# Two FFN stages of a diffusion layer: four raw weight buffers, later stores, resident output weights, and sums spread over the next product

## The chip, the cores and the metric

The kernel runs on one core of one Trainium2 chip. The core has TensorE (PE, with its weight loads shown apart as PEld), VectorE (DVE), ScalarE (ACT), GpSimd (POOL) and SyncE (SP), which here issues the DMA transfers. The time is device microseconds of one execution; a kernel's time is the median of several runs. Each kernel also has one execution with the hardware profiler on, and all rows of a profile belong to that execution.

## The reference

One layer for 1,024 latent tokens (x_sample) and 256 context tokens (x_prompt), model width 1,024, in float32. Two gated FFNs of inner width 2,816 stand around a token-mixing step; the change touches the FFNs only.

```python
def swiglu(h, w_in, w_out):
    gate, up = jnp.split(h @ w_in, 2, axis=-1)
    return (jax.nn.silu(gate) * up) @ w_out

def layer(x, cond, p, ...):
    ...
    h = rms_norm(x, p['norm_ffn1']) * (1.0 + sc1) + sh1
    x = x + 0.5 * g1 * swiglu(h, p['w_ffn1_in'], p['w_ffn1_out'])
    h = rms_norm(x, p['norm_mix']) * (1.0 + sc2) + sh2
    mix, k_ctx, v_ctx, s_ctx = token_mix(h, p, ...)
    x = x + g2 * mix
    h = rms_norm(x, p['norm_ffn2']) * (1.0 + sc3) + sh3
    x = x + 0.5 * g3 * swiglu(h, p['w_ffn2_in'], p['w_ffn2_out'])
```

w_in is 1,024 x 5,632, w_out 2,816 x 1,024. The vectors sh, sc and g come from the conditioning.

## The kernel before

Activations lie with the model dimension on the 128 partitions, eight tiles of 128 rows (`x[c][d]`); the tokens are three chunks: c = 0 and 1 are the latents (512 each), c = 2 is the prompt (256). Each float32 operand is split into a high part (`copy` to fp32r on ScalarE) and a low part (`subtract` on VectorE or GpSimd), and each product is three matmuls: high by high, high by low, low by high (`mm3`, line 129). So every weight tile is loaded, cast, subtracted, and only then used.

The program is written with a tile framework that finds the dependencies, allocates buffers by tag and puts each engine's instructions into an order of its own: by the order of the program among what is ready. It can issue a transfer long before the place where it is written, but each engine's queue, SP's too, is then run in that fixed order. A pool opened in the place of a closed one takes over its memory. Only the attention part is pinned to program order. `K.side` holds generators of side work (norms, operand splits, outputs); `tick` (line 114) advances each by one step between pieces of the main work.

One FFN (`ffn`, line 1392) has four stages.

1. *Prompt in* (`prompt_in`, line 468). For each of the NF = 22 tiles of inner width it takes a gate weight tile (g, 1,024 x 128, 512 KB) and an up tile (u), makes 24 matmuls of 256 columns with each, applies Silu on ScalarE, multiplies on VectorE, and stores the result s to DRAM (`gp_d`) for the fourth stage. Weights come by `wload` (line 88): raw tile (tag wr, two buffers), cast by ScalarE to wh, low part wl by VectorE (g) or GpSimd (u), four buffers each. `ahead(2)` keeps two converted tiles ready. Side work meanwhile makes the operands of the latents.
2. *Latents in* (`in_blocks` line 514, `latents_in` line 555). The latents' product is a 2 x 2 block scheme with seven products in place of eight (`prod`). For p = 0 to 10 (NPR = 11 pairs of inner tiles) and gate and up (u = 0, 1), it makes the seven products on operand tiles that stay on chip in pool `hp` (tags hh0, hl0, hh1, hl1, hh2, hl2) and in the x buffers, then seven combinations per pair are stored to DRAM (`g_d`). The weight blocks of this stage lie in pool `fp`.
3. *Latents out* (`out_blocks` line 623, `latents_out` line 656). Seven products again, in the order i = 1, 2, 5, 6, 7, 4, 3. Each runs over the 11 pairs p; a pair is 12 matmuls of 512 columns into four PSUM banks. For each pair a raw tile of two halves is loaded: g (256 KB of `g_d`) and a (256 KB of w_out), with a second piece of w_out for i = 5 and 7 (tag wr2). Products 5, 6, 7 and 3 use sums or differences of weight quarters. The raw tile is in tag wr (two buffers, kept through the kernel) or, for every third, wr3 in this stage's own pool `op`. `block` (line 488) casts and splits each half: a on GpSimd, g on VectorE. After a product, all its sums into x (`scalar_tensor_tensor`, one of 512 columns per bank and quarter of x, 4 to 16 per product) are written one behind the other; where a quarter of x is final, `done` starts its sum of squares (FFN1) or its output (FFN2). x itself was stored to DRAM while its memory held operands, and is loaded again before this stage: 4 MB of the latents, and 1 MB of the prompt's (`x_move`, tile xr).
4. *Prompt out* (`prompt_out_blocks` line 679, `prompt_out` line 692). For each of 22 tiles: w_out rows (512 KB), v (the stored s), split both, 24 matmuls of 256 columns.

After FFN1 comes the mixing step with its own projections, which also take their weights by `wload`.

## Time and profile before

| what | us |
|---|---|
| median of 3 runs | 2931.68 (2926.15 to 2934.43) |
| the profiled execution | 2935.67, span 2933.8 |
| FFN1: prompt in, latents in, latents out, prompt out start at | 41.6, 229.9, 705.7, 964.6 |
| FFN2: the same | 2022.8, 2187.4, 2615.4, 2862.4 |
| last matmul of FFN2's prompt out | 2927.7 |

Starts are those of the stage's first matmul, from the span's start. VectorE is busy for 1628.4 us of the span, GpSimd for 1265.5, ScalarE for 1122.1. A row of the timeline gives start, duration, engine, operation, the tiles written and read, and in brackets how long the engine had stood before it and what ended that. In names, numbers of buffers are left out: ffn2w_3g is the g block of pair 3 in any of the seven products, ffn2w_3b its weight block, ffn2w_3r the raw tile, ffn2u12r, h and l are raw, high and low part of up tile 12.

### The profile page before, as it was taken

The numbers are of one execution on the slowest core, as the hardware profiler recorded it, in microseconds if no ns is written. First come the engines' busy times: TensorE is split into PE (matmuls) and PEld (weight loads), VectorE is DVE, ScalarE is ACT, GpSimd is POOL, SyncE is SP. The second block draws the span as 40 slices with busy tenths as digits, with TensorE's granted clock in tenths as the row PEclk, the third lists the DMA queues.
The fourth block names the chain that finished last, engine by engine and source line by source line (L and its number), as shares of the span: only waits on it lengthen the run. The fifth ranks groups of instructions, "written<-read, shape, count | busy, mean of one in ns | idle before, by whom it ended". The sixth has DMA issues, their size and how long they took to land.

```text
span 2933.8 us, 44077 instructions
## 1 busy us (share of the span) xinstructions
PE 2732.8 (93%) x17070; PEld 2359.7 (80%) x17070; DVE 1628.4 (56%) x2162; ACT 1122.1 (38%) x1892; POOL 1265.5 (43%) x902
## 2 busy tenths in 40 slices
PE   6889999998989899999998999999889999989899
PEld 5776667886767798999988888888777888867789
DVE  4824344554676735464646388737525555546654
ACT  5532223332434533232323477735332333323344
POOL 2334334443445646455655112165335444434443
PEclk8999999999999899999999999999999999999999
DMA  8556664335665541313132954375553333256665
GB/s 300 164 156 193 208 205 140 108 101 191 220 196 197 184 156 48 110 58 107 54 98 84 222 116 110 129 248 158 151 147 93 108 108 108 90 195 217 202 215 194
DMA packets 420600, 446.62 MB, mean 152 GB/s; under 512 B 21549, under 2 KB 315685, under 8 KB 417317
## 3 DMA queue, kind: packets, MB, share of 16 engines
q1 hardware_dynamic: 420208, 443.73, 48.5%
q8 instruction: 134, 2.20, 0.3%
q14 instruction: 78, 0.63, 0.1%
q10 hardware_dynamic: 180, 0.06, 0.0%
HBM read 344.09 MB, written 99.61 MB: 151 GB/s over the span
## 4 chain that ended last, share of the span: by engine, by line
PE 63%; DVE 9%; DMA 8%; POOL 5%; issue 4%; ACT 2%; SPq 1%; DVEq 0%; ACTq 0%; POOLq 0%
PE mob L49 3%; PE ffn2po L49 3%; PE ffn2pp L49 2%; PE ffn1po L49 2%; PE ffn1pp L49 2%; PE hi0b L49 1%; PE ak1b L49 1%; PE ak0b L49 1%; PE aq0b L49 1%; PE ada L49 1%; PE av1b L49 1%; PE hi1b L49 1%; PE hg1b L49 1%; PE hg0b L49 1%; SPq L49 1%
## 5 line engine op out<-in xcount | busy, mean ns | idle before, releaser
L49 PE MATMUL ffn1pp<-ffn1pvv,ffn1pw 128*128 128x256 f32 x528 | 69.2, 295 | 4.6 <-ACT ffn1pvv L49 4.6
L49 PEld LDWEIGHTS ffn1pp<-ffn1pvv,ffn1pw 128*128 128x128 f32 x528 | 68.0, 203 | 5.8 <-ACT ffn1pvv L49 4.9
L49 PE MATMUL ffn2pp<-ffn2pvv,ffn2pw 128*128 128x256 f32 x528 | 64.0, 283 | 0.0
L49 PEld LDWEIGHTS ffn2pp<-ffn2pvv,ffn2pw 128*128 128x128 f32 x528 | 63.6, 192 | 0.1
L49 PE MATMUL ada<-wada,cst 128*32 128x256 f32 x448 | 39.8, 395 | 4.0 <-DMA wada<-w_ada 3.9
L49 POOL TENSOR_TENSOR ffn2pw<-ffn2pw,ffn2pw 128x512 fp32r<-128x512 f32 x22 | 28.9, 1316 | 33.6 <-ACT ffn2pw L49 29.7
L49 POOL TENSOR_TENSOR ffn1pw<-ffn1pw,ffn1pw 128x512 fp32r<-128x512 f32 x22 | 31.2, 1424 | 21.0 <-ACT ffn1pw L49 20.9
L49 PE MATMUL ffn1po<-ffn1w_3g,ffn1w_3b 128*128 128x512 f32 x84 | 25.7, 453 | 11.9 <-DVE ffn1w_3g L49 11.9
L49 DVE TENSOR_TENSOR sacc<-sacc,sq 128x512 f32<-128x512 f32 (+1 forms) x18 | 27.0, 1500 | 15.7 <-ACT sq L49 15.5
L49 ACT CAST ffn1pw<-ffn1pw 128x512 fp32r<-128x512 f32 x44 | 25.8, 616 | 23.2 <-DMA ffn1pw<-w_ffn_out 21.4
L49 PE MATMUL ffn1po<-ffn1w_2g,ffn1w_2b 128*128 128x512 f32 x84 | 23.5, 430 | 11.9 <-ACT ffn1w_2b L49 11.6
L49 ACT CAST ffn2pw<-ffn2pw 128x512 fp32r<-128x512 f32 x44 | 26.8, 620 | 18.1 <-DMA ffn2pw<-w_ffn_out 12.0
L49 PE MATMUL ffn2po<-ffn2w_2g,ffn2w_2b 128*128 128x512 f32 x84 | 23.4, 427 | 11.0 <-ACT ffn2w_2b L49 10.7
L49 PE MATMUL ffn2po<-ffn2w_3g,ffn2w_3b 128*128 128x512 f32 x84 | 24.3, 439 | 9.2 <-DVE ffn2w_3g L49 9.2
L49 POOL TENSOR_TENSOR hl<-nt,hh 128x256 fp32r<-128x256 f32 (+1 forms) x20 | 22.5, 1127 | 24.0 <-ACT hh L49 24.0
L49 ACT ACTIVATE nt<-nt,mt,sv 128x256 f32<-128x256 f32 (+1 forms) x40 | 25.5, 681 | 18.8 <-DVE nt L49 11.5
L49 PEld LDWEIGHTS ffn1po<-ffn1w_3g,ffn1w_3b 128*128 128x128 f32 x84 | 18.2, 223 | 18.0 <-DVE ffn1w_3g L49 14.0
L49 DVE TENSOR_TENSOR ffn2pw<-ffn2pw,ffn2pw 128x512 fp32r<-128x512 f32 x22 | 18.0, 817 | 25.9 <-ACT ffn2pw L49 25.9
L49 PEld LDWEIGHTS ffn1po<-ffn1w_2g,ffn1w_2b 128*128 128x128 f32 x84 | 17.0, 207 | 17.2 <-ACT ffn1w_2b L49 12.0
L49 PEld LDWEIGHTS ada<-wada,cst 128*32 128x32 f32 x448 | 9.8, 108 | 25.7 <-issue 19.3
L49 PEld LDWEIGHTS ffn2po<-ffn2w_2g,ffn2w_2b 128*128 128x128 f32 x84 | 16.7, 206 | 16.0 <-ACT ffn2w_2b L49 11.1
L49 DVE TENSOR_TENSOR ffn1pw<-ffn1pw,ffn1pw 128x512 fp32r<-128x512 f32 x22 | 20.6, 936 | 16.1 <-ACT ffn1pw L49 13.6
(4022 smaller groups left out, 10296.8 us busy)
## 6 DMA issues: line engine op xcount, KB each, us to landing
wada<-w_ada SPq DMA_DIRECT2D x112, 256.0 KB, 3.0
ffn1r<-w_ffn_in SPq DMA_DIRECT2D x44, 512.0 KB, 4.3
ffn2r<-w_ffn_in SPq DMA_DIRECT2D x44, 512.0 KB, 3.8
ffn1pw<-w_ffn_out SPq DMA_DIRECT2D x22, 512.0 KB, 4.5
ffn2pw<-w_ffn_out SPq DMA_DIRECT2D x22, 512.0 KB, 3.3
g_d<-ffn1t SPq DMA_DIRECT2D x33, 256.0 KB, 2.8
g_d<-ffn2t SPq DMA_DIRECT2D x33, 256.0 KB, 2.9
wadb<-w_ada SPq DMA_DIRECT2D x12, 512.0 KB, 8.8
```

What stands on the lines that cost most here:

```text
L49: r = f(*a, **k)
```

## The change

In the prompt stage, raw weight tiles come from four buffers, two of wr and two of a new tag wrx in another pool, with up to three loads issued ahead of their cast (`rload`, `nraw`); elsewhere one load is issued ahead (`nraw = 1`). Three converted tiles are kept ready in place of two. The store of s for step f - 1 is written after the product of step f.

In latents out, the w_out quarters of the first 512 columns (a11, a12: 22 tiles of 256 KB) are put into the memory of operands hh0, hl0, hh2, hl2, and stay there through the stage. Eight of them are loaded from within the last step of latents in, the others in the stage. Products 6, 7 and 3 take them from there, and no longer load them. g tiles come from a tag gr with four buffers in pool `op`, loaded two pairs ahead of their split; weights for products 5, 7 and 4 by the shared raw buffers. x is loaded in eight pieces of 512 KB written between the pairs' loads, and the prompt's x during product 5. The order of the products is 1, 2, 5, 6, 7, 3, 4. The sums into x of a product are a generator, two sums per tick, in the course of the next product. Prompt out loads two tiles ahead, v through tag gr.

```diff
+    def rload(self):
+        src, name = self.wq.popleft()
+        self.nr += 1
+        pool, tag = (self.xraw, "wrx") if self.xraw is not None and self.nr % 2 else (self.wp, "wr")
+        raw = pool.tile(list(src.shape), F32, tag=tag, bufs=2, name=name + "r")
+        self.nc.sync.dma_start(raw, src)
+        self.rawq.append((raw, name))
 def wload(self):
-        src, name = self.wq.popleft()
-        raw = self.wp.tile(shape, F32, tag="wr", bufs=2, name=name + "r")
-        nc.sync.dma_start(raw, src)
+        if not self.rawq:
+            self.rload()
+        raw, name = self.rawq.popleft()
...
+        while len(self.rawq) < self.nraw and self.wq:
+            self.rload()
 def prompt_in(self, tp, name):
-            self.ahead(2)
+            self.ahead(3)
...
-            nc.sync.dma_start(self.gp_d[:, f], s)
+            if late is not None:
+                nc.sync.dma_start(self.gp_d[:, f - 1], late)
+            late = s
 def latents_in(self, fp, name, pop, after):
+                if p == NPR - 1 and u:
+                    after()
                 b3 = self.bank(n_ + "p3")
                 prod(b3, "22")
...
-            if p == NPR - 2:
-                after()
+    def out_resident(self, hp, wout, name):
+        t = [hp.tile([P, m, 512], F32, tag=g, name=f"{name}q{g}") for m, g in ((8, "hh0"), (8, "hl0"), (4, "hh2"), (2, "hl2"))]
+        fl = [x[:, j] for x, m in zip(t, (8, 8, 4, 2)) for j in range(m)]
+        self.a11, self.a12 = fl[:NPR], fl[NPR:]
 def out_blocks(self, wout, name, hp, xp, pool):
+        def load(j):
...
+            g = pool().tile([P, 512], F32, tag="gr", bufs=4, name=n_ + "gr")
+            nc.sync.dma_start(g, self.g_d[:, i - 1, p])
+            a = None
+            if i == 1:
+                if p >= 8:
+                    self.out_w(wout, self.a11[p], p, 0, 0)
+            elif i == 2:
+                self.out_w(wout, self.a12[p], p, 0, 1)
+            elif i in (5, 7, 4):
+                a = self.raw(pool, [P, 2, 512], n_ + "r")
...
+            if xs and j >= 2 and j % 2 == 0:
+                nc.sync.dma_start(*xs.popleft())
+            if i == 5 and p == 4:
+                self.x_move(pool(), 2, True)
+        load(0)
+        load(1)
+        for j, (i, p) in enumerate(keys):
+            load(j + 2)
...
 def latents_out(self, name, pop, g, ng, done, then):
+        def drain(i, bs):
+            n = 0
+            for h, c in C[i]:
+                for d in range(4):
...
+                    nc.vector.scalar_tensor_tensor(x, bs[d], m, x, op0=ALU.mult, op1=ALU.add)
...
+                    n += 1
+                    if n % 2 == 0:
+                        yield
...
+            ds.append(drain(i, bs))
+            self.side.append(ds[-1])
+        then()
+        for q in ds:
+            self.finish(q)
 def ffn(st, name, which, hp, xp, side, nxt, done):
+        def after():
+            K.out_resident(hp, wout, name)
+            for p in range(8):
+                K.out_w(wout, K.a11[p], p, 0, 0)
         K.half = True
+        K.xraw, K.nraw = st["raw"](), 3
         K.prompt_in(st["t"], name)
...
+        K.xraw, K.nraw = None, 1
...
             ao(2)
-            for c in (0, 1):
-                K.x_move(xp, c, True)
-            K.x_move(op, 2, True)
```

Before FFN2, `K.xraw` and `nraw = 3` are set already in the output projection of the mixing step (chunk 0, from its third tile on).

More of the change, by code (lines that the diff above doesn't have):

```diff
@@ L616, in latents_in, with raw @@
                 nc.sync.dma_start(self.g_d[:, i, p], t)
[L617 to L623 removed]
+    def raw(self, pool, shape, name):
+        self.nr += 1
+        if self.nr % 3 == 2:
+            return pool().tile(shape, F32, tag="wr3", bufs=1, name=name)
+        return self.wp.tile(shape, F32, tag="wr", bufs=2, name=name)
@@ new lines, in out_blocks @@
+        s_ = None
+        load(0)
+        load(1)
+        for j, (i, p) in enumerate(keys):
+            load(j + 2)
+            g, a = raws.pop(j)
+            n_ = f"{name}w{i}_{p}"
+            if i == 5 and p == 0:
+                s_ = [hp.tile([P, m, 512], F32, tag=t, name=f"{name}s{t}") for m, t in ((8, "hh1"), (3, "hl1"))]
+                s_ = [s_[0][:, q] for q in range(8)] + [s_[1][:, q] for q in range(3)]
+            if i == 1:
+                a = self.a11[p]
+            elif i == 2:
+                a = self.a12[p]
+            elif i == 5:
+                V.tensor_tensor(s_[p], a[:, 0], a[:, 1], op=ALU.add)
+                a = s_[p]
+            elif i == 6:
+                V.tensor_tensor(s_[p], s_[p], self.a11[p], op=ALU.subtract)
+                a = s_[p]
+            elif i == 7:
+                V.tensor_tensor(self.a11[p], self.a11[p], a[:, 0], op=ALU.subtract)
+                a = self.a11[p]
+            elif i == 3:
+                V.tensor_tensor(self.a12[p], self.a12[p], s_[p], op=ALU.subtract)
+                a = self.a12[p]
+            else:
+                a = a[:, 1]
+            yield self.block(a, n_ + "b", G), self.block(g, n_ + "g", V)
@@ L670, in latents_out, with load @@
                 self.tick()
-            for d in range(4):
-                for h, c in C[i]:
-                    x = self.x[c][4 * h + d]
-                    m = (ng if i == 4 else g)[:, 4 * h + d, 0:1]
-                    nc.vector.scalar_tensor_tensor(x, bs[d], m, x, op0=ALU.mult, op1=ALU.add)
-                    if last.get(i) == (h, c):
-                        done(c, 4 * h + d)
+            ds.append(drain(i, bs))
[3 more added lines that the diff above has]
+            self.finish(q)
     def prompt_out_blocks(self, wout, name, pool):
         nc = self.nc
+        raws = {}
+        def load(f):
+            if f < NF:
+                r = self.raw(pool, [P, D], f"{name}pw{f}")
+                nc.sync.dma_start(r, wout[0, f * P:(f + 1) * P, :])
+                v = pool().tile([P, NP], F32, tag="gr", bufs=4, name=f"{name}pv{f}")
+                nc.sync.dma_start(v, self.gp_d[:, f])
+                raws[f] = r, v
+        load(0)
+        load(1)
         for f in range(NF):
-            r = self.raw(pool, f, [P, D], f"{name}pw{f}")
-            nc.sync.dma_start(r, wout[0, f * P:(f + 1) * P, :])
-            v = pool().tile([P, NP], F32, tag="gp", bufs=3, name=f"{name}pv{f}")
-            nc.sync.dma_start(v, self.gp_d[:, f])
+            load(f + 2)
+            r, v = raws.pop(f)
             w = [self.block(r[:, h * 512:(h + 1) * 512], f"{name}pw{f}{h}", nc.gpsimd if h else nc.vector)
@@ L1496, in nxt @@
                 pv.close()
[L1497 removed]
+            ffn({"t": qp, "raw": lambda: qp, "close": q1.close, "side": lambda: K.side.append(adas()), "end": ta.close},
                 "ffn1", 0, hp, xp, "right", nxt, done1)
```

85 lines of the change are left out of this document (44 added, 41 removed).

## The prediction, made before the changed kernel was built or run

> **What bounds the kernel now.** I read the first part of the page, then busy time by stage, then, where TensorE is not full, the waits of PE and the timeline.
>
> ```profile
> span 2933.8 us, 44077 instructions
> ...
> PE 2732.8 (93%) x17070; PEld 2359.7 (80%) x17070; DVE 1628.4 (56%) x2162; ACT 1122.1 (38%) x1892; POOL 1265.5 (43%) x902
> ```
>
> PE is the bound, so only time in which PE stands or runs slowly can be won. The table by stage (busy us and instructions of each engine, granted clock, DMA share, GB/s) finds it. In order: FFN1's prompt stage in three stretches, FFN2's likewise, a stretch of FFN2's input products, the two output stages (FFN1, FFN2), the two prompt-output stages.
>
> ```profile
> core 0: us, PE busy (x) PEld busy (x) DVE busy (x) ACT busy (x) POOL busy (x), PEclk, DMA share, GB/s
> 41.60:99.90 58.30, 44.50 (x302) 41.46 (x303) 37.30 (x53) 34.07 (x59) 16.54 (x8) 0.88 0.71 239
> 99.90:146.80 46.90, 37.50 (x266) 35.47 (x266) 41.40 (x50) 23.81 (x37) 17.17 (x5) 0.92 0.46 136
> 146.80:230.00 83.20, 68.32 (x531) 65.55 (x530) 16.97 (x22) 27.16 (x34) 28.58 (x13) 0.98 0.54 158
> 2022.80:2057.00 34.20, 34.20 (x284) 33.61 (x283) 28.39 (x35) 22.30 (x32) 13.30 (x6) 1.00 0.58 179
> 2057.00:2101.80 44.80, 35.12 (x267) 33.45 (x265) 31.25 (x38) 19.53 (x29) 14.28 (x6) 0.96 0.50 147
> 2101.80:2187.40 85.60, 69.29 (x531) 66.51 (x530) 18.25 (x21) 26.25 (x34) 28.52 (x13) 0.96 0.54 153
> 2250.00:2600.00 350.00, 350.00 (x1546) 289.82 (x1545) 194.01 (x255) 112.18 (x187) 167.33 (x129) 1.00 0.31 99
> 705.70:964.80 259.10, 226.86 (x945) 180.42 (x944) 168.00 (x210) 104.66 (x179) 121.36 (x84) 0.95 0.63 208
> 2615.40:2862.60 247.20, 223.84 (x975) 181.33 (x974) 148.85 (x192) 94.25 (x165) 108.20 (x78) 0.96 0.67 220
> 964.60:1045.50 80.90, 72.15 (x549) 70.79 (x549) 51.73 (x68) 43.08 (x81) 47.78 (x33) 0.92 0.57 192
> 2862.40:2927.70 65.30, 65.30 (x547) 65.24 (x546) 29.23 (x51) 30.00 (x59) 26.27 (x20) 1.00 0.61 197
> ```
>
> The input products show PE without a gap: 350 us / 1546 = 0.2264 us per matmul of 512 columns. The first stretch of FFN2's prompt stage gives 34.2 / 284 = 0.1204 us per matmul of 256. With these, the work of a stage is known from the code. A weight tile (24 matmuls) is 2.89 us; the stretches hold 11, 11 and 22 tiles, 31.8, 31.8 and 63.6 us. Above that stand 26.5, 15.1 and 19.6 us in FFN1 and 2.4, 13.0 and 22.0 us in FFN2. An output stage is 7 x 11 x 12 = 924 matmuls, 209.2 us, so FFN1's has 49.9 us above that and FFN2's 38.0 (3.6 of it are the 64 transposes of 128 columns for y, at the rate of the columns, which stay). FFN1's prompt-output stage takes 15.6 us more than FFN2's same one. These are about 200 us in all; nothing else that the change touches has PE waiting for weights.
>
> **Prompt stages: four raw buffers, later stores.** One turn of the loop in FFN2, in order of time (start, duration, engine, what, what ended its wait):
>
> ```profile
> 2106.48 0.37 SPq L49 DMA_DIRECT2D ffn2u12r<-w_ffn_in  x1
> ...
> 2106.99 1.23 DVE L49 TENSOR_TENSOR ffn2g12l<-ffn2g12r,ffn2g12h 128x1024 fp32r<-128x1024 f32 x1 [4.51 <-ACT ffn2g12h L49]
> ...
> 2109.93 0.34 SPq L49 DMA_DIRECT2D gp_d<-ffn2s  x1
> ...
> 2111.42 1.05 ACT L49 CAST ffn2u12h<-ffn2u12r 128x1024 fp32r<-128x1024 f32 x1 [4.18 <-DMA ffn2u12r<-w_ffn_in]
> ...
> 2112.55 2.35 POOL L49 TENSOR_TENSOR ffn2u12l<-ffn2u12r,ffn2u12h 128x1024 fp32r<-128x1024 f32 x1 [6.10 <-ACT ffn2u12h L49]
> ...
> 2114.96 0.58 PE L49 MATMUL ffn2pu<-hh,ffn2u12l 128*128 128x256 f32 x1 [1.93 <-POOL ffn2u12l L49]
> ```
>
> A raw tile is requested only when one of two buffers is free. u12 is requested at 2106.48, cast at 2111.42 (4.94 us later), its low part made by GpSimd in 2.35 us, and PE starts that low part at 2114.96 after 1.93 us of standing. The turn from request to free buffer is 4.94 + 1.05 + 2.4 = 8.4 us and two buffers carry the two tiles of a 5.78 us step of PE. So the load turn-around is the bound. The store at 2109.93 stands in SP's queue between two loads:
>
> ```profile
> SPq L49 <- DVE ffn2s L49: 17.1, 8, 3.3
> ```
>
> In 60 us SP stood 17.1 us, in 8 places, for the product that a store takes, with the next load behind it. Four buffers give 4 / 8.4 us, over twice the rate, and the store of the step before never makes SP wait. Then the slowest work per step is PE's 5.78 us: GpSimd has 2.35, ScalarE two casts of 1.05 and one Silu, VectorE 1.23 and a product; DMA moves 1.18 MB, 205 GB/s, where output stages already show 220. FFN2's last stretch goes from 22.0 to about 1 us over, its middle one from 13.0 to 4 (VectorE, 31 of 45 us busy, still makes operands there): **30 us**. Bounds: 12 if only the last stretch's half goes, 35 if all goes.
>
> FFN1's last stretch gives 18.6 the same way. Its middle stretch has VectorE busy 41.4 of 46.9 us; if that work keeps its place PE can't get below it, so 5.5. The first stretch holds these waits for weights (us, times, longest):
>
> ```profile
> PE ffn1pu L49 <- ACT ffn1u1h L49: 3.5, 1, 3.5
> ...
> PE ffn1pg L49 <- ACT ffn1g5h L49: 2.5, 1, 2.5
> ...
> PE ffn1pu L49 <- POOL ffn1u1l L49: 1.6, 1, 1.6
> ```
>
> They are 7.7 us, and 9 with the slow clock that follows (below): 18.6 + 5.5 + 9 = **33 us**, bounds 18 and 50. The extra raw load during the prologue may delay it by one 512 KB load, under 2 us; it is in these bounds. In the projections after FFN1, one tile is now requested earlier; PE waits for no weight there, so nothing.
>
> **The start of the output stage.** FFN2, VectorE's and SP's side and PE's:
>
> ```profile
> 2587.28 0.40 SPq L49 DMA_DIRECT2D ffn2w_1r<-g_d  x1
> ...
> 2612.61 0.32 SPq L49 DMA_DIRECT2D xr1a<-xd  x1
> ...
> 2615.36 2.88 PE L49 MATMUL ffn2po<-ffn2w_0g,ffn2w_0b 128*128 128x512 f32 x12
> ...
> 2621.15 0.94 SPq L49 DMA_DIRECT2D g_d<-ffn2t  x2
> ...
> 2622.13 1.29 SPq L49 DMA_DIRECT2D xr<-xd  x2
> ...
> 2623.47 0.45 SPq L49 DMA_DIRECT2D ffn2w_2r<-g_d  x1
> ...
> 2629.92 0.62 ACT L49 CAST ffn2w_2g<-ffn2w_2r 128x512 fp32r<-128x512 f32 x1 [24.57 <-DMA ffn2w_2r<-g_d]
> ...
> 2631.63 1.22 PE L49 MATMUL ffn2po<-ffn2w_2g,ffn2w_2b 128*128 128x512 f32 x2 [10.66 <-ACT ffn2w_2b L49]
> ...
> 2637.13 2.88 PE L49 MATMUL ffn2po<-ffn2w_3g,ffn2w_3b 128*128 128x512 f32 x12
> ```
>
> The first two pairs were loaded ahead through the buffers that outlive the stage change (2587.28), so PE starts at 2615.36 at once; the third needs the stage's own pool, whose loads stand on SP right behind the last stores of the pool before (2621.15), lands 6.45 us after its request, and PE stands 10.66 us. FFN1 has the same (its first and fourth pair):
>
> ```profile
> 705.66 2.88 PE L49 MATMUL ffn1po<-ffn1w_0g,ffn1w_0b 128*128 128x512 f32 x12
> ...
> 728.67 2.89 PE L49 MATMUL ffn1po<-ffn1w_3g,ffn1w_3b 128*128 128x512 f32 x12
> ```
>
> From the first to the fourth pair: 21.77 us and 23.01 us where three pairs need 8.15, so 13.6 and 14.9 lost. In the changed code every product tile g comes from the stage's own pool (tag gr), the first pair's too. If its loads keep their place behind those stores, PE stands from the very first pair. Least: the 1 MB of xr (2622.13) no longer stands ahead; at the queue's rate (from 2612.61 to 2629.92 it moved 2 MB of x, six stores of 256 KB, xr and the pair's half, 4.98 MB in 17.3 us, 288 GB/s) that is 3.6 us, so g lands 2.8 us after 2622.1, PE starts 1.7 later (2629.92 to 2631.63 before), and the fourth pair comes at 2626.6 + 8.15 + 2.78 = 2637.5, 0.4 later than now. Most: all resident weights (22 x 256 KB, 5.77 MB) and x stand ahead, since their buffers come free product by product from 2615.36 - 6 x 2.72 = 2599.0 on; less xr and the early pairs' 1.05 MB each, and with 2.1 us more time, g lands 10.7 us later than 2629.92, and the fourth pair comes 16.4 us later than now. SP can't issue them all before its stores fall due, so I take half of the weights ahead: **6 us lost** in each FFN. Both ends stay in the range, and below nothing too: if gr came free as early as 2600, the 13.6 and 14.9 us would go.
>
> The slow clock is in these sums: the pair after the 10.66 us took 5.50 us (2631.63 to 2637.13) for 2.72. The Trainium skill, "TensorE: Matmul & The Clock Gate" (Part 1, The HAM clock gate), gives half rate for about 3.4 us after an idle window of about 3.4 us, by which the loss would be about 1.7 us, an estimate, and not the 2.78 measured; and by it the next wait, under 3.4 us, would cost no more than itself, where this trace shows more:
>
> ```profile
> 2670.61 3.63 PE L49 MATMUL ffn2po<-ffn2w_3g,ffn2w_3b 128*128 128x512 f32 x8 [2.49 <-DVE ffn2w_3g L49]
> ```
>
> Eight matmuls took 3.63 us for 1.81 after a wait of 2.49. I take the rows.
>
> **Sums into x spread out.** The output stages stop at the fourth pair of a product, behind VectorE (FFN2's row; FFN1 shows the same place):
>
> ```profile
> PE ffn2po L49 <- DVE ffn2w_3g L49: 9.2, 3, 4.8
> ```
>
> ```profile
> L49 DVE SCALAR_TENSOR_TENSOR xr1b<-ffn2po,mt,xr1b 128x512 f32<-128x512 f32 x16 | 11.8, 735 | 0.0
> ...
> L49 DVE TENSOR_TENSOR ffn2w_7g<-ffn2w_7r,ffn2w_7g 128x512 fp32r<-128x512 f32 x6 | 6.6, 1096 | 5.1 <-ACT ffn2w_7g L49 2.7 <-PE ffn2po L49 2.5
> ```
>
> After a product VectorE does 4 to 16 sums of 0.735 us in a row, and the split of a pair's g stands behind them. Spread by two per pair, VectorE has 1.47 + 1.10 of split, and as much again for a sum of weights in four products: 2.6 to 3.7 us against 2.72, for at most eight pairs, with three pairs made ahead (8.2 us), so the row absorbs it. FFN2's loss outside its start is 38.0 - 3.6 - 13.6 = 20.8; I leave 7 (the transposes' own waits, small ones): **14 won**, bounds 6 and 18. FFN1's is 49.9 - 14.9 = 35.0; the norms of both chunks, with their own waits and VectorE work, stay: I leave 17, **18 won**, bounds 9 and 25. Weight transfers of 256 KB fall from 99 to 66 per FFN, 8.65 MB less; outside the start PE waits for no load, so nothing more. The order 3 before 4 exchanges which chunk's norm falls into the prompt-output stage.
>
> **Prompt output.** Two tiles loaded ahead, and v through gr:
>
> ```profile
> PE ffn1pp L49 <- ACT ffn1pvv L49: 4.6, 1, 4.6
> ```
>
> FFN1 gets this 4.6 us and some of its slow clock back, **6 us** (0 to 10); FFN2's has no loss.
>
> **Sum.** 30 + 33 - 12 + 14 + 18 + 6 = 89 us. The profiled execution took 2935.67 us (span 2933.8 and 1.87 around it), so 2846.7; it lies 4.0 above the median of 2931.68, so I predict 2842.7 beside that.
>
> **Rivals.** *Resident weights block the start fully.* For it: buffers free from 2599.0, and 1 MB transfers issued at 2612.61 and 2622.13 did delay the pair at 2623.47. Against it: SP needs 0.3 to 0.7 us per issue and has stores between. 16.4 instead of 6.0 twice: 68 us won, 2863. The Trainium skill, "DMA: Bandwidth & Descriptors" (Two DMAs through the same engine are not ordered), says descriptors of one queue on one engine start in order; by it whatever SP issues first does go first, and the 4.98 MB in 17.3 us agree.
>
> *The start gap closes.* For it: gr might lie where the raw tiles of the input products end early; against it: all loads of the new pool came together behind 2621.15. 89 + 12 + 28.5 = 129.5 won, 2802.
>
> *The prompt stages gain half.* The change then doesn't do what it says: the queue's order is made by readiness, so a store may still stand ahead of a load, and VectorE's operands hold the low parts back. For it FFN1's 41.4 of 46.9; against it FFN2's first stretch, full with 28.4 of 34.2. 31.5 less: 57.5 won, 2874.
>
> *Slower: the ring of four gr tiles becomes the bound of the output stages.* A turn is landing + cast 0.62 + split 1.1; at four tiles it limits a pair once the landing exceeds 4 x 2.72 - 1.7 = 9.2 us; at 12 us a pair takes 3.43, 0.71 more, 54.7 per stage, 109 in all, and the kernel is 20 slower, 2952; it passes zero at 11.5 us. For it: x, weights and g share one queue, as at 2623.47. Against: even that one took 6.45.
>
> **How the numbers follow.** Forecast 0.45, blocked start 0.20, half the prompt gain 0.16, closed start 0.13, slower 0.06. 0.3% (9 us) is about what a measurement of this kernel can tell from no change. The first four are all faster; 0.01 of the slower case may fall within 0.3%. The range takes the blocked start, half gain with a few us of the other bounds, and the closed start: 2797 to 2885.
>
> **What would show it.** Prompt stages of about 134 us (FFN2) and 155 (FFN1), the SP queue's waits for ffn2s gone, and PE's waits for low parts of u gone. At the output stage, PE standing before its first pair, from the end of the input products until about 10 to 17 us later. No wait of PE for w_3g at product changes. Wrong would be: prompt stages above 150 us in FFN2; a first pair without a gap; waits of PE for g in the middle of products.

## The result and the profile after

| | before | after |
|---|---|---|
| median, us | 2931.68 | 2850.30 (2845.98 to 2855.65, 4 runs) |
| the profiled execution, us | 2935.67, span 2933.8 | 2853.46, span 2851.6 |

The ratio is 0.9726, 95% interval 0.9701 to 0.975: faster. The forecast was 2842.7, the range 2797 to 2885.

The first part of the page of the changed kernel (busy us, share of the span, instructions):

```profile
span 2851.6 us, 43957 instructions
...
PE 2699.0 (95%) x17070; PEld 2343.7 (82%) x17070; DVE 1655.1 (58%) x2162; ACT 1117.3 (39%) x1892; POOL 1288.7 (45%) x902
```

PE issues the same 17,070 matmuls and has 82 us less of span around them. The table by stage of the changed kernel, with the columns of the prediction's table and in its order (FFN1's prompt stage in three stretches, FFN2's, the two output stages), then FFN1's prompt output and the mixing step. Output stages run here from the end of the input products, so that the stop ahead of the first pair lies in them.

```profile
44.20:87.60 43.40, 39.95 (x301) 38.31 (x302) 28.71 (x42) 29.39 (x54) 15.12 (x7) 0.94 0.89 287
87.60:133.50 45.90, 37.07 (x267) 35.97 (x266) 45.90 (x55) 27.88 (x44) 20.41 (x6) 0.89 0.60 163
133.50:196.80 63.30, 63.30 (x530) 63.30 (x529) 21.10 (x28) 24.82 (x33) 28.98 (x12) 1.00 0.67 187
1972.30:2006.30 34.00, 34.00 (x283) 33.50 (x282) 29.00 (x33) 23.84 (x34) 13.80 (x6) 1.00 0.65 196
2006.30:2048.00 41.70, 33.84 (x266) 33.19 (x265) 34.05 (x42) 19.50 (x30) 21.55 (x6) 0.92 0.58 163
2048.00:2110.70 62.70, 62.70 (x531) 62.70 (x530) 15.67 (x20) 24.38 (x32) 26.50 (x12) 1.00 0.62 180
670.60:915.20 244.60, 220.48 (x942) 180.43 (x943) 170.41 (x201) 100.12 (x177) 122.53 (x83) 0.94 0.56 182
2538.10:2779.80 241.70, 219.86 (x974) 179.68 (x974) 164.97 (x196) 93.38 (x165) 112.75 (x76) 0.96 0.59 189
915.20:1000.20 85.00, 71.28 (x548) 69.45 (x547) 58.17 (x78) 45.76 (x84) 49.82 (x33) 0.92 0.55 181
1000.20:1972.30 972.10, 933.46 (x7416) 860.95 (x7415) 565.78 (x750) 408.31 (x690) 428.71 (x319) 0.99 0.42 120
```

Read the PE column against the length of the stretch. The last stretches of both prompt stages are full (63.3 of 63.3, 62.7 of 62.7; before 68.3 of 83.2 and 69.3 of 85.6). The middle ones are not: VectorE fills FFN1's (45.9 of 45.9). FFN1's prompt-output stage has become longer (85.0 us; before 80.7 from first matmul to the next stage's first).

The load turn-around of the prompt stage in FFN2, in order of time, for a tile like the one of the prediction:

```profile
2051.67 0.37 SPq L49 DMA_DIRECT2D ffn2u14r<-w_ffn_in  x1
...
2059.52 1.05 ACT L49 CAST ffn2u14h<-ffn2u14r 128x1024 fp32r<-128x1024 f32 x1 [1.56 <-issue]
...
2060.64 2.40 POOL L49 TENSOR_TENSOR ffn2u14l<-ffn2u14r,ffn2u14h 128x1024 fp32r<-128x1024 f32 x1 [3.31 <-ACT ffn2u14h L49]
```

u14 is requested 7.85 us ahead of its cast, where u12 before had 4.94, and in this stretch ScalarE's casts wait for no transfer any more. The waits of SP in those 60 us, in which SP stood 17.1 us for ffn2s before:

```profile
SPq L49 <- DVE ffn2s L49: 8.0, 11, 0.8
```

SP still stops at every store, 11 times in 60 us. The stops have become harmless, not absent.

The start of FFN2's output stage:

```profile
2544.38 0.32 SPq L49 DMA_DIRECT2D g_d<-ffn2g10x  x1
...
2546.25 0.43 SPq L49 DMA_DIRECT2D ffn2w_0gr<-g_d  x1
...
2551.85 0.62 ACT L49 CAST ffn2w_0g<-ffn2w_0gr 128x512 fp32r<-128x512 f32 x1 [15.70 <-DMA ffn2w_0gr<-g_d]
...
2552.52 5.77 PE L49 MATMUL ffn2po<-ffn2w_0g,ffn2w_0b 128*128 128x512 f32 x12 [14.36 <-ACT ffn2w_0g L49]
...
2558.13 2.24 PE L49 MATMUL ffn2po<-ffn2w_1g,ffn2w_1b 128*128 128x512 f32 x9
```

As forecast, the first g tile is requested behind the last store of the stage before (2544.38), and PE stands 14.36 us ahead of its first pair; that pair then takes 5.61 us (2552.52 to 2558.13) for 2.72.

All waits of PE for pairs in FFN1's output stage (us, times, longest), and the three of FFN1's prompt-output stage for its own operands:

```profile
PE ffn1po L49 <- ACT ffn1w_0g L49: 15.4, 1, 15.4
PE ffn1po L49 <- DVE ffn1w_10g L49: 3.5, 1, 3.5
PE ffn1po L49 <- DVE ffn1w_5g L49: 3.1, 1, 3.1
PE ffn1po L49 <- POOL ffn1w_4b L49: 2.5, 1, 2.5
```

```profile
PE ffn1pp L49 <- ACT ffn1pvv L49: 4.4, 1, 4.4
PE ffn1pp L49 <- DVE ffn1pw L49: 4.0, 2, 3.3
PE ffn1pp L49 <- DVE ffn1pvv L49: 3.8, 1, 3.8
```

No wait for w_3g is left; three in product 5 are new. In the prompt-output stage the 4.6 us that were to go are still there (4.4), with two more kinds beside them.

### The profile page after: what moved, and what is told of

It is laid out like the page before. It is cut to its first block, busy times and chain, and to the rows that moved or that the text cites. A ratio compares the mean times of both kernels' runs of the same rounds, so it can differ in the third digit from the quotient of the medians.

```text
span 2851.6 us, 43957 instructions
## 1 busy us (share of the span) xinstructions
PE 2699.0 (95%) x17070; PEld 2343.7 (82%) x17070; DVE 1655.1 (58%) x2162; ACT 1117.3 (39%) x1892; POOL 1288.7 (45%) x902
## 4 chain that ended last, share of the span: by engine, by line
PE 74%; DVE 7%; POOL 4%; DMA 3%; issue 3%; ACT 1%; SPq 0%; POOLq 0%; DVEq 0%; ACTq 0%
PE ffn2po L49 6%; PE ffn1po L49 6%; PE mob L49 4%; PE ffn2pp L49 2%; PE ffn2pu L49 2%; PE ffn2pg L49 2%; PE ffn1pp L49 1%; PE aq0b L49 1%; PE ak1b L49 1%; PE ak0b L49 1%; PE ada L49 1%; PE av1b L49 1%; PE hi1b L49 1%; PE ffn1u4p L49 1%; PE hg0b L49 1%
## 5 line engine op out<-in xcount | busy, mean ns | idle before, releaser
L49 PE MATMUL ffn1po<-ffn1w_0g,ffn1w_0b 128*128 128x512 f32 x84 | 23.5, 432 | 15.4 <-ACT ffn1w_0g L49 15.4
L49 PE MATMUL ffn2po<-ffn2w_0g,ffn2w_0b 128*128 128x512 f32 x84 | 23.6, 430 | 14.9 <-ACT ffn2w_0g L49 14.4
L49 PEld LDWEIGHTS ffn1po<-ffn1w_0g,ffn1w_0b 128*128 128x128 f32 x84 | 17.8, 214 | 20.2 <-ACT ffn1w_0g L49 15.8
L49 PEld LDWEIGHTS ffn2po<-ffn2w_0g,ffn2w_0b 128*128 128x128 f32 x84 | 17.1, 207 | 20.2 <-ACT ffn2w_0g L49 14.8
L49 DVE TENSOR_TENSOR sacc<-sacc,sq 128x512 f32<-128x512 f32 (+1 forms) x18 | 26.9, 1493 | 10.7 <-ACT sq L49 10.4
L49 DVE TENSOR_TENSOR ffn2pw<-ffn2pw,ffn2pw 128x512 fp32r<-128x512 f32 x22 | 17.0, 772 | 25.8 <-ACT ffn2pw L49 25.8
L49 DVE TENSOR_TENSOR ffn1pw<-ffn1pw,ffn1pw 128x512 fp32r<-128x512 f32 x22 | 19.9, 905 | 14.2 <-ACT ffn1pw L49 14.1
L49 DVE TENSOR_REDUCE a_0mx<-a_0S 128x1 f32<-128x1536 f32 x8 | 14.1, 1758 | 24.3 <-DMA a0k<-k_d 12.8
L49 POOL TENSOR_TENSOR nr<-nm,nh 128x4 f32<-128x4 f32 (+1 forms) x9 | 8.7, 962 | 40.2 <-DVE nm L49 40.2
L49 PE MATMUL ffn1po<-ffn1w_5g,ffn1w_5b 128*128 128x512 f32 x84 | 22.1, 413 | 3.1 <-DVE ffn1w_5g L49 3.1
```

What stands on the lines that cost most here:

```text
L49: r = f(*a, **k)
```

## The experiments

Ratios are to the kernel before, run on the same chip; the changed kernel stands at 0.9726. Stages are from each profiled execution, one per kernel. The mixing step took 965.8 to 973.0 us among the ten kernels that keep loads ahead in it, though most edits between them lie elsewhere; a few us of a long stage are therefore no difference.

**1. Two raw buffers.**

```diff
-        K.xraw, K.nraw = st["raw"](), 3
+        K.xraw, K.nraw = None, 1
...
-                hq["p"] = K.xraw = q1.enter_context(K.pool("q2h"))
-                K.nraw = 3
+                hq["p"] = q1.enter_context(K.pool("q2h"))
```

> The changed kernel with the raw weight tiles from the two old buffers again and one load ahead (no tag wrx); later stores, three converted tiles and all of the output stages stay. Theory, the load turn-around of two buffers was the bound of the prompt stages: FFN2's goes from 138.4 us back to about 160, FFN1's from 152.8 to about 183, and the kernel is 45 to 60 us slower than the changed one, 2895 to 2910, 0.988 to 0.993 of before. Rival, the later stores gave the gain: both stages within 8 us of the changed kernel's, the kernel at most 15 slower, and the rows of SP waiting for ffn2s stay absent.

2906.16 us, ratio 0.9934 (0.9917 to 0.9951). FFN2's prompt stage and FFN1's:

```profile
1998.30:2165.80 167.50, 141.46 (x1076) 136.85 (x1075) 74.79 (x93) 68.08 (x95) 57.48 (x24) 0.94 0.52 153
44.10:222.50 178.40, 147.16 (x1094) 141.54 (x1095) 93.47 (x123) 83.18 (x129) 54.62 (x25) 0.93 0.59 184
```

FFN2's stage is 3 us longer than before (164.6). So the two added buffers and their early loads carry all of FFN2's gain, and 25.8 us of FFN1's stage; later stores, a third converted tile and one load ahead alone give FFN2 nothing. FFN1's stage ends 7.4 us earlier than before without the added buffers (222.5 for 229.9); which of the three does that isn't separated. In FFN2 the stores do come later here: from the ninth to the 21st they stand about 2.1 us behind their product and behind the next u load, where before all but three follow the product at once. SP's waits for them fall from 31.5 to 12.1 us in the stage, and the time doesn't follow.

**2. Stores at their old place.**

```diff
-            if late is not None:
-                nc.sync.dma_start(self.gp_d[:, f - 1], late)
-            late = s
+            nc.sync.dma_start(self.gp_d[:, f], s)
...
-        nc.sync.dma_start(self.gp_d[:, NF - 1], late)
```

> The changed kernel with the store of s for step f written right behind the product of step f, as before; four raw buffers stay. Theory, buffers are the bound: up to three loads stand ahead, a store that holds SP for some 3 us is covered, so FFN2's prompt stage stays at 138 to 143 us, FFN1's at 152 to 160, the kernel 0 to 12 us slower than the changed one (0.972 to 0.977 of before). Rival, stores ahead of loads were the larger part: FFN2's stage goes to 150 or more, the kernel is 20 to 35 us slower (0.98 to 0.985).

2843.72 us, ratio 0.9728 (0.9693 to 0.9764); FFN2's stage takes 138.5 us and FFN1's 153.0 (138.4 and 152.6 in the changed kernel). That looks like a store whose place is worth nothing, but the edit hardly moved it. The store behind one step's product in FFN2, first in the changed kernel, then in this run:

```profile
2054.40 0.34 SPq L49 DMA_DIRECT2D gp_d<-ffn2s  x1
```

```profile
2044.22 0.34 SPq L49 DMA_DIRECT2D gp_d<-ffn2s  x1
```

The products that these stores take start at 2053.95 and 2043.77 and last 0.42 us: in both kernels the store is issued as soon as its product is ready, between the same two loads (g15 and u15), and so it is along FFN2's stage. In FFN1 only the first five stores stand later in the changed kernel, by 2 to 10 us, and the stage is 0.4 us shorter. The order of the queue goes by readiness, so a store written one step later need not be issued later. What differs from the kernel before is that the loads around a store are two tiles further ahead (g13 and u13 before). The run shows that writing the store later is worth nothing. What a store that really stands later is worth with four buffers stays open; in run 1, with two, it gave FFN2 nothing. In the prediction both were one term, and the buffers and their early loads carry it.

**3. Sums in a row.**

```diff
-            ds.append(drain(i, bs))
-            self.side.append(ds[-1])
+            if i == 1:
+                ds.append(drain(i, bs))
+                self.side.append(ds[-1])
+                continue
+            while ds:
+                self.finish(ds.popleft())
+            for _ in drain(i, bs):
+                pass
```

> The changed kernel with the sums into x of the products 2, 5, 6, 7, 3 and 4 written in a row behind each product again (those of product 1 stay spread, since x is not yet loaded by then). Theory, the sums in a row made the stops at product changes: PE waits again for the split of g at about the fourth pair of products 5, 6, 7 and 4 (w_3g), 15 to 26 us over both FFNs, the kernel at 0.977 to 0.982 of before. Rival, the resident weights and the g tiles loaded two pairs ahead removed those stops: no more than 5 us, 0.972 to 0.975. The prompt-output stage of FFN1 (85.0 us in the changed kernel) shows on the side what late sums cost there: by the theory that late sums push the norms into it, it falls back towards 80.7.

2847.44 us, ratio 0.9728 (0.9692 to 0.9765). The rival's number. FFN1's output stage, its prompt output, FFN2's output stage:

```profile
670.00:920.00 250.00, 223.72 (x943) 181.84 (x944) 184.61 (x209) 104.26 (x183) 127.55 (x87) 0.94 0.54 178
920.00:996.30 76.30, 70.86 (x549) 69.59 (x548) 50.09 (x71) 41.84 (x77) 42.45 (x28) 0.93 0.60 201
2532.10:2774.00 241.90, 221.35 (x974) 181.09 (x974) 166.09 (x196) 93.43 (x165) 103.49 (x76) 0.96 0.57 188
```

FFN2 doesn't change (241.7 to 241.9). FFN1's output stage is 5.4 us longer, its prompt output 8.7 shorter. So in this kernel the spread of all products but the first is worth nothing, and costs 3.3 us in FFN1. The sums of product 1, the longest row (16), stay spread here, so this run doesn't say what they would do. Why the row no longer stops PE is seen on the timeline after product 6 of FFN2 (the first PE row of each is the next product's first pair); first before, then this run:

```profile
2759.64 2.88 PE L49 MATMUL ffn2po<-ffn2w_0g,ffn2w_0b 128*128 128x512 f32 x12
...
2763.18 1.13 DVE L49 TENSOR_TENSOR ffn2w_3r<-ffn2w_3r,ffn2w_3r 128x512 f32<-128x512 f32 x1 [2.14 <-DMA ffn2w_3r<-w_ffn_out]
2764.23 0.74 DVE L49 SCALAR_TENSOR_TENSOR xr1a<-ffn2po,mt,xr1a 128x512 f32<-128x512 f32 x1
...
2772.74 0.67 DVE L49 TENSOR_TENSOR ffn2w_3g<-ffn2w_3r,ffn2w_3g 128x512 fp32r<-128x512 f32 x1
```

```profile
2678.72 0.75 DVE L49 SCALAR_TENSOR_TENSOR xr1a<-ffn2po,mt,xr1a 128x512 f32<-128x512 f32 x1 [0.81 <-PE ffn2po L49]
...
2680.56 2.88 PE L49 MATMUL ffn2po<-ffn2w_0g,ffn2w_0b 128*128 128x512 f32 x12
...
2687.80 1.00 DVE L49 TENSOR_TENSOR ffn2w_3g<-ffn2w_3gr,ffn2w_3g 128x512 fp32r<-128x512 f32 x1
...
2688.72 2.96 PE L49 MATMUL ffn2po<-ffn2w_3g,ffn2w_3b 128*128 128x512 f32 x12
```

Before, VectorE stands for a weight transfer and starts its row 4.6 us after PE has begun the next product; the split of w_3g comes 8.5 us after the row's start, and PE waits 4.8 us for it. In this run VectorE waits for PE, starts its first sum 1.8 us before the next product, and 9.1 us later the split comes just in time: PE takes up w_3g at 2688.72 without a wait. The row is as long as it was. At this change of products, its start had been late.

**4. First g tiles ahead.**

```diff
             for p in range(8):
                 K.out_w(wout, K.a11[p], p, 0, 0)
+                nc.sync.dma_start(K.a12[p], K.g_d[:, 0, p])
...
-            g = pool().tile([P, 512], F32, tag="gr", bufs=4, name=n_ + "gr")
-            nc.sync.dma_start(g, self.g_d[:, i - 1, p])
+            if j < 8:
+                g = self.a12[p]
+            else:
+                g = pool().tile([P, 512], F32, tag="gr", bufs=4, name=n_ + "gr")
+                nc.sync.dma_start(g, self.g_d[:, i - 1, p])
```

> The changed kernel with the g tiles of the first eight pairs of product 1 loaded from within the last step of latents in, into the memory of the resident weights for product 2 (which are loaded over them later), so that they need neither the stage's own pool nor a place behind the last stores. Theory, the stop of PE ahead of the first pair (15.4 us in FFN1, 14.4 in FFN2, and the slow pair behind it, 2.7 and 2.9) is the place of the g loads on SP's queue: it goes, and at most a few us come back later, so 25 to 35 us less than the changed kernel, 0.961 to 0.964 of before. Rival, the queue is full of resident weights and x, so the start is bound by bytes: PE stands just as long, or the same time again in pairs 2 to 8, and the kernel is within 10 us of the changed one, 0.97 to 0.973.

2814.83 us, ratio 0.9623 (0.9591 to 0.9656). FFN2's start:

```profile
2501.71 2.22 SPq L49 DMA_DIRECT2D ffn2qhl<-g_d  x5
...
2512.40 2.88 PE L49 MATMUL ffn2po<-ffn2w_0g,ffn2w_0b 128*128 128x512 f32 x12
```

The g tiles are requested from 2501.71 on, and the stop is gone. The output stages take 226.8 and 225.3 us, 17.8 and 16.4 less than in the changed kernel; the bytes are the same. So the place of the g loads, in memory and in the queue, was the cause, and the bytes were not the bound.

**5. The spread alone, on the kernel before.** The generator of the change in the loop of before, in the old order of products (its core):

```diff
-            for d in range(4):
-                for h, c in C[i]:
-                    ...
+            ds.append(drain(i, bs))
+            self.side.append(ds[-1])
+        then()
+        for q in ds:
+            self.finish(q)
```

> The kernel before with one part of the change alone: the sums into x of a product are spread by two per pair over the following product (order of products, raw buffers, weights and loads as before). First theory, the sums in a row made the stops: the waits of PE for w_3g go (9.2 us in FFN2 with the slow pairs behind them), 10 to 18 us per FFN, the kernel at 0.989 to 0.993 of before. Second theory, formed after the run with sums in a row: the stop needs two things, a row of sums and VectorE standing for a weight piece's DMA ahead of that row (in FFN2 before, the sums of product 6 start 4.4 us after the product's end, behind differences of weights that wait for their transfers); spreading alone takes one of them away and also suffices for most of it, 6 to 12 us per FFN, less 8 us in FFN1's prompt-output stage for the later norms. Rival, the spread does nothing here: within 5 us of before.

2907.01 us, ratio 0.9947 (0.9929 to 0.9965). FFN1's output stage, its prompt output, FFN2's output stage:

```profile
704.00:944.40 240.40, 222.14 (x943) 176.47 (x942) 164.56 (x206) 103.72 (x181) 120.83 (x84) 0.96 0.68 226
944.40:1030.00 85.60, 72.47 (x549) 71.06 (x548) 55.99 (x72) 42.54 (x79) 49.73 (x34) 0.90 0.54 177
2597.90:2833.30 235.40, 221.08 (x974) 179.41 (x973) 146.63 (x191) 91.85 (x164) 104.71 (x76) 0.97 0.70 229
```

Against 258.9, 80.7 and 247.0 before: 18.5 and 11.6 won, 4.9 given back. No wait for w_3g is left. The spread alone takes these stops away, as the prediction said of it, and makes the prompt output longer by itself. Its worth is less sure than the stages say: they make 25.2 us, the medians on this chip 17.1, and the ratio lies between the first theory's 0.993 and the rival. The kernel before took 2916.8 to 2929.3 us on this chip and 2935.67 in its profile, so some 10 us of the difference need not be the spread's. With run 3: for the products after the first, either the spread or the rest of the change removes most of these stops, and the second to come adds nothing.

**6. Row, and no resident weights in products 6, 7 and 3.** The row of run 3, and

```diff
-            elif i in (5, 7, 4):
+            else:
                 a = self.raw(pool, [P, 2, 512], n_ + "r")
+                if i in (6, 7):
+                    self.out_w(wout, a[:, 0], p, 0, 0)
...
-                V.tensor_tensor(s_[p], s_[p], self.a11[p], op=ALU.subtract)
+                V.tensor_tensor(s_[p], s_[p], a[:, 0], op=ALU.subtract)
```

and likewise for 7 and 3.

> The changed kernel with two parts undone at once: the sums of products 2, 5, 6, 7, 3 and 4 stand in a row again, and products 6, 7 and 3 load their quarters of the output weights again through the raw tiles (wr and wr3) instead of taking the resident ones; g by four tiles of its own and two pairs ahead stays. Theory that row and weight transfers together make the stops: PE's waits for w_3g to w_5g at product changes return, 15 to 25 us over both FFNs against the run with the row alone (2847 us), the kernel at 0.978 to 0.981 of before. Rival, the g tiles loaded two pairs ahead through four buffers removed the stops, and the resident weights do nothing: within 5 us of 0.9728.

2845.50 us, ratio 0.9729 (0.9704 to 0.9754): the rival's time again. FFN1's output stage 251.4 (250.0 in run 3), FFN2's 239.4 (241.9). In time, the 66 transfers saved per kernel bought nothing. But in FFN1 the theory's stops are back, where run 3 has none:

```profile
PE ffn1po L49 <- DVE ffn1w_3g L49: 4.6, 2, 2.4
```

They stand at the changes from product 5 to 6 and from 7 to 3. VectorE has loaded weights to combine again (at the first change it waits 2.04 us for one), its first sum comes 3.5 us after the start of the next product (0.6 and 1.8 us ahead of it in run 3), and the split of w_3g 10.2 and 10.0 us after (5.3 and 5.7). Against that the stops in product 5 of FFN1, 8.3 us in run 3, are down to 0.6. So the second theory holds at these two places, and the resident weights take one stop away and make another; the time can't show either.

**7. Order 4, 3.**

```diff
-    OUT = (1, 2, 5, 6, 7, 3, 4)
+    OUT = (1, 2, 5, 6, 7, 4, 3)
```

> The changed kernel with product 4 ahead of product 3 again, sums spread. Theory, late sums and not the order cost FFN1's prompt-output stage its 4.3 us (85.0 us; 76.4 with the sums in a row): the stage stays at 83 to 87 us and the kernel within 4 us of the changed one, 0.971 to 0.974 of before. Rival, the order pushes the second norm into that stage: it falls to 76 to 80 us, the kernel at 0.9695 to 0.971.

2855.28 us, ratio 0.9768 (0.9748 to 0.9789). The ratio lies above what either theory gave. FFN1's prompt output takes 88.8 us, 3.8 more than in the changed kernel (the theory had 83 to 87, the rival 76 to 80), and the span is 2.3 us longer; the rest of the difference in ratio shows in no stage, and the changed kernel wasn't run on this chip. So the order is not what costs there, the old one is rather worse. The cause is shown by all the kernels together: the five with the last products' sums in a row (runs 3, 6, 9, 10, 11) take 75.1 to 76.3 us in this stage, the seven with all sums spread (the changed one, runs 1, 2, 4, 5, 7, 8) 84.5 to 88.8. Late sums start the norms later.

**8. No load ahead outside the prompt stages.**

```diff
-        K.xraw, K.nraw = None, 1
+        K.xraw, K.nraw = None, 0
...
-                hq["p"] = K.xraw = q1.enter_context(K.pool("q2h"))
-                K.nraw = 3
+                hq["p"] = q1.enter_context(K.pool("q2h"))
```

> The changed kernel with no raw load ahead outside the two prompt stages (nraw = 0 there, and no third and fourth raw buffer in the output projection of the mixing step). Theory, the 5.2 us that the mixing step gained are these loads (two to three tiles in the token projections, 1.4 us each, and 2.8 us in the output projection): 4 to 6 us slower than the changed kernel, the step back at 976 to 978 us. Rival, they are the order of the instructions or chance: the step stays at 971 to 974 us.

2853.32 us, ratio 0.9763 (0.9744 to 0.9783). The mixing step of before, and of this run:

```profile
1045.30:2022.80 977.50, 937.80 (x7416) 864.95 (x7415) 563.27 (x750) 408.74 (x690) 428.31 (x319) 0.98 0.41 118
```

```profile
995.70:1973.10 977.40, 936.60 (x7415) 863.52 (x7414) 562.80 (x749) 408.08 (x689) 427.06 (x319) 0.98 0.41 120
```

The changed kernel had 972.1. The three kernels without a load ahead (before, runs 5 and 8) take 976.5 to 977.5 us here, the ten with one 965.8 to 973.0. So the loads ahead shorten the mixing step; by how much is open, since the ten differ by more than the 5.4 us among themselves. Run 1, which keeps one load ahead but not the further buffers, has 972.7 us (1025.6 to 1998.3): the one load is enough. By which path is open too, since PE waits for no weight there in either kernel; 4.3 of the 5.4 us are PE's busy time (937.8 to 933.5), not its waits.

**9, 10. Combinations.** Both have the edit of run 4, and the sums of products 3 and 4 in a row (`if i in (3, 4):` ahead of the row of run 3). Run 9 adds the weights of run 6; run 10 keeps the resident ones and adds squares on VectorE (`nc.vector` for `(nc.vector if h else nc.gpsimd)` in `sumsq`).

> The changed kernel with three edits: the first eight g tiles ahead (as in the fourth run, 2814.8 us), the sums of the last two products (3 and 4) in a row, and products 6, 7 and 3 loading their quarters of the output weights again through the raw tiles. Theory: the resident quarters let VectorE do weight differences of later products ahead of the g splits of product 5, which is why PE stops there (w_4g, w_5g, w_10g in FFN1, some 14 us above 2.72 each; w_7g to w_0g in FFN2, some 8); with raw tiles the stops of product 5 go, as in the sixth run, and with spread sums no others come; the sums in a row at the end give back 5 to 8 us of FFN1's prompt-output stage and cost up to 6 in the output stage. 2785 to 2800 us, 0.953 to 0.957 of before. Rival: those stops come from the bytes and GpSimd alone, and 66 transfers more of 256 KB make others: 2810 to 2825, 0.961 to 0.966.

> The changed kernel with the first eight g tiles ahead, the sums of products 3 and 4 in a row, and all additions of squares (sacc) on VectorE; the resident weights stay. Theory of GpSimd: in FFN1's product 5 three additions of squares take GpSimd 6.93 us in a row ahead of the low part of w_4b, and VectorE's next weight difference waits for that; on VectorE they take 0.7 us each, and the stops at w_4g and w_10g of FFN1 go (5 to 10 us), FFN2's stay (it has no squares). 2798 to 2808 us, 0.957 to 0.960 of before. Theory of the resident differences alone (as for the run beside it): the stops stay, 2808 to 2816, 0.960 to 0.963.

Run 9: 2803.01 us, ratio 0.9579 (0.9558 to 0.96), the fastest here. Run 10: 2814.03, 0.9614 (0.9597 to 0.9632). FFN1's output stage, its prompt output and FFN2's output stage in run 9:

```profile
669.00:894.80 225.80, 217.58 (x943) 176.65 (x942) 186.13 (x206) 102.67 (x180) 129.24 (x87) 0.98 0.71 236
894.80:969.90 75.10, 69.69 (x549) 68.42 (x547) 50.23 (x72) 40.83 (x76) 42.41 (x27) 0.95 0.62 205
2506.80:2728.60 221.80, 218.19 (x973) 180.24 (x972) 163.37 (x193) 91.14 (x162) 107.13 (x76) 0.98 0.74 245
```

Run 9 falls between its theory and its rival, run 10 where the resident differences had it. Against run 4 (226.8, 85.9, 225.3) most of run 9's gain is the prompt output, by 10.8 us, from the last rows; 1.0 and 3.5 come in the output stages, where 14 and 8 had been hoped for. The theory of run 9 was right about two stops all the same. In the changed kernel VectorE waits in FFN1's product 5 for GpSimd, whose low part of w_4b still reads the tile that a difference for product 6 overwrites:

```profile
762.29 1.76 DVE L49 TENSOR_TENSOR ffn1shh<-ffn1shh,ffn1qhh 128x512 f32<-128x512 f32 x1 [5.12 <-POOL ffn1w_4b L49]
```

It then makes four sums and differences, this one the first, of 1.75 to 1.77 us (0.68 where it runs alone) ahead of the split of w_5g. In run 9 the stops at w_5g and w_10g are gone and PE's waits in FFN1's product 5 fall from 8.8 us in run 4 to 3.1; but with the last products' sums in a row PE stands 4.0 us for w_9g of the last product (3.3 to 3.5 in runs 3, 6 and 10).

Run 10's output stages take 232.3 and 223.7, and PE still waits 3.2 us for w_4b. GpSimd's additions are not the cause by themselves. In run 10, GpSimd's own low part is slow:

```profile
739.36 5.86 POOL L49 TENSOR_TENSOR ffn1w_4b<-ffn1shh,ffn1w_4b 128x512 fp32r<-128x512 f32 x1 [1.30 <-ACT ffn1w_4b L49]
```

It took 1.26 us in the changed kernel. VectorE, which has the additions now, runs without a pause until 744.1, and GpSimd ends at 745.2. What the kernels share is GpSimd beside a VectorE that doesn't stop (see the last section); no run takes that away, so this cause is read from the rows and not shown.

**11. Two g tiles in place of four**, on run 6.

```diff
-            g = pool().tile([P, 512], F32, tag="gr", bufs=4, name=n_ + "gr")
+            g = pool().tile([P, 512], F32, tag="gr2", bufs=2, name=n_ + "gr")
```

> The run with the sums in a row and without the resident weights in products 6, 7 and 3 (the sixth, 0.9729 of before, stages of 236.4 and 224.5 us) with two g tiles in place of four. Theory, four g tiles of their own are what took the product changes' stops away beside the spread: with two, PE's waits for w_2g to w_4g after each product return, 8 to 25 us over both FFNs, 0.976 to 0.982 of before. Rival, they do nothing, and the order of products or the transfers freed of g did it: within 4 us of the sixth run.

2852.52 us, ratio 0.9745 (0.9723 to 0.9767). The output stages take 253.1 and 245.7 us, 1.7 and 6.3 more than in run 6. The ratios of runs 6 and 11 overlap in their intervals, so the rows alone tell them apart. PE's waits for w_3g are no longer in FFN1 than in run 6 (4.7 us in 4 places, 4.6 in 2); in FFN2, where run 6 has none:

```profile
PE ffn2po L49 <- DVE ffn2w_3g L49: 2.6, 2, 1.3
```

So the depth of the g ring may be part of what made the row harmless, a small one. The rest isn't separated: raw tiles that hold only weights, loads written two pairs ahead, product 1 spread.

## Why the prediction was right, and where it was wrong

| term | forecast, us won | profile |
|---|---|---|
| FFN2 prompt in | 30 | 164.6 - 138.4 = 26.2 |
| FFN1 prompt in, with the prologue | 33 | 229.9 - 196.8 = 33.1 |
| start of the output stages, FFN1, FFN2 | -6, -6 | -3.2, -3.7 |
| sums, FFN1, FFN2 | 18, 14 | 17.5, 9.0 |
| prompt output FFN1 | 6 | 80.7 - 85.0 = -4.3 |
| mixing step | 0 | 977.5 - 972.1 = 5.4 |

The start is the stop plus what the first pair takes over 2.72 us: 14.36 + 2.89 = 17.25 in FFN2, against 13.6 before; 15.39 and a pair of 5.46 us in FFN1, against 14.9. The sums are the rest of the stage: 247.0 - 241.7 + 3.7 and 258.9 - 244.6 + 3.2. The terms make 80.0; FFN1's input products, which nothing touches, are 2 us shorter (2 to 4 in the other kernels too, run 5 included). The spans differ by 82.2. That the sum came within 9 us of the forecast is in part luck: three terms were 4 to 10 us too high, the two stage starts lost 2 to 3 us less than forecast, and the 5.4 us of the mixing step were not in the sum.

*Prompt stages.* The bound and half of the cure were right: the turn-around of two buffers, shown by run 1. The last stretches gave 22.9 and 19.9 (21 and 18.6 forecast). FFN2's middle stretch gave 3.1 of 9: VectorE is busy for 34.1 of its 41.7 us, and one low part on GpSimd took far longer than its usual time (last section). FFN1's first stretch gave 14.9 in place of 9, less 2.6 for a prologue that ends later (under 2 forecast), and its middle stretch 1.0 in place of 5.5: there VectorE's 41.4 us were taken as the floor, but more of its work fell into the stretch, 45.9 of 45.9 us. So FFN1's exact 33 is luck. Wrong was the sentence that "the store of the step before never makes SP wait", and with it the sign that the waits of SP for ffn2s would be gone. They are there, 28.0 us in FFN2's stage (31.5 before), since the queue goes by readiness and issues the store where it stood; the rival of half the gain had said that this might happen. It cost nothing: SP is only late where a load behind it is late, and the loads are now two tiles further ahead. The 17.1 us of SP's waiting had been read as a cost.

*Start of the output stage.* The mechanism was right: the stop moved from the third and fourth pair to the first, 14 to 15 us long, and lost little. Run 4 shows that it was the loads' place. What the weights ahead cost was priced too high. More than half of them stood in front: in each FFN 14 of the 22 resident weights and six pieces of x were requested ahead of the first g, but 12 of the 14 more than 15 us ahead of it (in FFN2 by 2531.0, g at 2546.25), and g landed 5.6 us after its request in FFN2, where the pair of before took 6.45. By the prediction's own terms the fully blocked start is 16.1 us later and not 16.4 (2629.92 + 10.7 + 1.7 + 8.15 + 2.78 against 2637.13), which changes nothing.

*Sums.* The size was right in FFN1, by luck, since 9.1 us of new stops in product 5 are in it that the forecast didn't have; it was 5 too high in FFN2, where new stops of 7.5 us stand in product 5 and at the start of 6. The reason was right for the kernel before (run 5), but not unique: in the changed kernel the stops behind all products but the first stay away without the spread (run 3). I had read the row's length as the cause. It is, alone, behind the 16 sums of product 1: there the first sum comes 0.9 and 0.6 us ahead of the next product, and PE still waits 2.2 and 2.5 us. The other five stops at w_3g stand behind rows of 8 and 12 that start 1.5 to 5.0 us after the next product has begun, so there VectorE's late start is as much of it; in FFN1 run 6 brings back both, the late start and the stop, at two of these places.

*Prompt output, the step that failed.* "FFN1 gets this 4.6 us and some of its slow clock back, 6 us (0 to 10)": 4.3 us lost. With the sums in a row the stage is 4.4 us shorter than before (76.3 us in run 3), which may be the two tiles loaded ahead, though run 3 differs in more; with the sums spread they bring nothing (85.0 us against 85.6 in run 5 without them). The spread delays the last sums, with them the sums of squares and the norms, and VectorE and ScalarE do these while PE needs their splits: 8.7 us between run 3 and the changed kernel, 4.9 in run 5. VectorE is busy for 58.2 us of the stage in place of 50.1 in run 3. The prediction looked at which chunk's norm falls into that stage; run 7 shows that the new order doesn't cost the time, since the old one takes 3.8 us more.

*Mixing step.* "PE waits for no weight there, so nothing": true of the waits, wrong of the time. Run 8 ties a gain there to the loads; its size and path stay open.

*Rivals.* The blocked start and the closed start are excluded by the 14 to 15 us; half the prompt gain by 26.2 and 33.1, though one of its grounds, the order by readiness, held. The 4.98 MB in 17.3 us that stand with the first rival are a rate, and show no order of transfers. The slower case, a ring of four g tiles as the bound, would show as waits for g from pair to pair; outside product 5 and the first pair of FFN2's product 6 (0.6 us) there are none.

## What to carry to other kernels

Count the turn from request to free buffer against the step of the engine that is the bound: where buffers are too few, more of them win nearly all of it, up to the next engine that is full. Waits of the issuing queue are no cost while the loads behind them are early enough. Where a framework orders a queue by readiness, look in the trace whether a statement that was moved has moved. Two cures of one stop don't add, so each part of a change is worth only what the others leave, and one that delays an end (a sum that a norm waits for) can cost more than it brings: spread early products, and finish the last ones at once. At a stage change, put the first loads into memory that is free before the old stage's last stores.

## What the runs showed of the hardware

GpSimd's low part of a 128 x 1,024 tile took 2.40 us in the steps of the prompt stage where VectorE has little to do (u14 above), and 7.74 us where VectorE ran without a pause. In the changed kernel:

```profile
2024.56 7.74 POOL L49 TENSOR_TENSOR ffn2u8l<-ffn2u8r,ffn2u8h 128x1024 fp32r<-128x1024 f32 x1 [6.65 <-ACT ffn2u8h L49]
...
2027.61 2.49 DVE L49 TENSOR_TENSOR o2l<-xr1a,o2t3h 128x512 f32<-128x512 f32 x4
...
2030.34 5.43 DVE L49 CAST o2t3l<-o2l 128x512 fp32r<-128x512 f32 x4
```

VectorE keeps its pace on subtractions of two tiles (2.49 us for four) while GpSimd gets nowhere. GpSimd ends at 2032.30, 2.2 us after the last of these subtractions, about the time that it needs by itself. Then it is VectorE that waits: of the four copies in the last row the first took 2.24 us and the second 2.60, each ending about 0.3 us after an instruction of GpSimd, the other two 0.42 each. PE waited 5.97 us for the low part, the largest stop that is left in FFN2's prompt stage. The Trainium skill, "SBUF — State Buffer" (Who interferes with whom), says that a VectorE instruction with two SBUF inputs contends with a GpSimd instruction that reads SBUF, and that the ports they share are an exclusive lock. These rows agree: 7.74 us against 2.40, and 2.24 and 2.60 against 0.42, one engine at a time.

The slow clock after a stop was again dearer than the rule that the prediction weighed: the pair after the 14.36 us took 5.61 us for 2.72, 2.89 over, at a granted clock of 0.50 (2552.5 to 2558.1), and the next pairs ran at 1.00. The Trainium skill, "TensorE: Matmul & The Clock Gate" (Part 1, The HAM clock gate), has half rate for about 3.4 us, which is an estimate of 1.7 us lost. The row decides.
